# Weight parts at turning start bytes in a float32r transformer layer

## The chip, the cores and the metric

The kernel runs on one core of one Trainium2 chip. The metric is the device time of one execution in microseconds (us). Three runs of the kernel before gave 1863.11, 1863.22 and 1865.91 us; the median is 1863.22 us. The profile comes from one more execution, which took 1856.3 us.

On the core, TensorE multiplies matrices. A matmul has a stationary operand, which is loaded first by a weight load, and a moving operand, which streams past it. The profile shows the matmuls as PE and the weight loads as PEld. ACT (ScalarE) and DVE (VectorE) do elementwise work, POOL (GpSimd) and SP (SyncE) mostly issue DMAs. Operands lie in the on-chip memory with 128 partitions; a tile takes the same bytes of every partition.

## The reference, cut to what matters

One transformer layer over 512 tokens with 2048 features: attention in a window of 128 tokens, then a swiglu with 5632 inner features.

```
h = rms_norm(x, mixer_norm)
x = x + sliding_window_attention(h, positions, w_qkv, q_norm, k_norm, sinks, w_o)
h = rms_norm(x, ffn_norm)
x = x + (silu(h @ w_gate) * (h @ w_up)) @ w_down
```

Everything is float32.

## The kernel before, in words

**Split products.** Every large product is done in float32r, a form of float32 that TensorE takes in one pass. Each operand is split into a high part (ACT copies the value, rounded to float32r) and a low part (DVE subtracts the high part from the value). A product is then three matmuls: high by high, high by low, low by high. All weight tiles come from memory by DMA as float32 and are split this way, and TensorE reads only the parts. `copy_r` and `sub` are the two helpers, so most rows of the profile for splits stand under their lines (L65 for ACT, L70 for DVE), and nearly all matmuls stand under the line of `mm` (L144).

**Stages.** The program goes in this order:

1. The qkv projection and the attention, interwoven by a table of events. Here the activations (`hhi`, `hlo`) are stationary and the weight parts (`whi`, `wlo`) move, 512 columns at a time.
2. The output projection. Its last 512 columns use eight pairs of weight parts that have their own pool: `ohi` and `olo`, 8 buffers each. They are made in `w_split`. Again the activations are stationary and the weight parts move. This stage has 4 token tiles of 16 row tiles of 3 matmuls, so 192 matmuls of 512 columns.
3. The first two units of the gate, with whole weight tiles (`whi`, `wlo` stationary, `hhi`, `hlo` moving).
4. The swiglu proper, from `unit` and `s_split`. It uses a fast matrix product of seven instead of eight block products. There are 168 steps. In each, `s_split(i)` makes a pair `Whi`, `Wlo` of [128, 2, 7, 128] in two buffers by turns, and TensorE does 2 x 7 x 3 = 42 matmuls with 128 weight columns stationary and 256 moving columns. So the stage has 168 x 42 = 7056 matmuls. Three of the seven products have `hhi`, `hlo` as the moving operand (18 of the 42 matmuls), four have the combinations `sh0` to `sh3` and `sl0` to `sl3` (24 of the 42).
5. The down projection, in three passes over the inner features, four times 512 output columns each. `d_split` makes the parts `dwh`, `dwl` of [128, 7, 256] in three buffers by turns. Here the activation is stationary (`sh`, `sl` in the first four steps of a pass and column group, `hhi`, `hlo` in the rest) and the weight parts move. For the first 512 columns of a pass the product is plain, with 24 matmuls of 512 moving columns a step; for the others it is the fast form, with 42 matmuls of 256 moving columns a step. That makes 288 matmuls with `sh`, `sl` and 240 with `hhi`, `hlo` of 512 columns, and 1512 and 1260 of 256 columns.

**Order.** TensorE's order is written out by hand throughout, and ACT's and DVE's from the last output columns on. Tiles in the pools are placed one after the other from a base address; a few `place` tiles in the down projection fix which tile lands where, so that early ones lie where the swiglu's buffers are already free.

**Where the parts begin.** All row lengths before are multiples of 512 bytes, so every part of one kind begins at the same byte modulo 512. In the built program these bytes are:

| Stage | stationary operand, byte modulo 512 | moving operand, byte modulo 512 |
|---|---|---|
| last output columns | `hhi`, `hlo`: 352 | `ohi`, `olo`: 480 |
| first gate units | `whi`, `wlo`: 352 | `hhi`, `hlo`: 352 |
| swiglu | `Whi`, `Wlo`: 352 | `hhi`, `hlo`: 352; `sh`, `sl`: 480 |
| down projection | `hhi`, `hlo`: 352; `sh`, `sl`: 480 | `dwh`, `dwl`: 352 |

A tile of 128 float32r columns is 512 bytes wide, so one weight load reads 512 bytes of a partition; 256 moving columns are 1024 bytes, 512 are 2048.

In the attention the transposes of the probabilities `p` have `p` itself as the stationary operand; its rows are 132 numbers long, so its blocks begin at eight different bytes, 16 apart (160 to 272 modulo 512).

Of the kernel before, what the change touches and what calls it, by code (L numbers as in the profile page):

```python
# [11 lines left out]
F32R = mybir.dt.float32r  # L12
# [7 lines left out]
P = 128  # L20
# [26 lines left out]
def hybrid_layer(ctx, tc, x, positions, inv_freq, mixer_norm, ffn_norm, w_qkv, q_norm, k_norm, sinks,  # L47
# [15 lines left out]
    def copy_r(dst, src, scale=None):  # L63
        if scale is None:
            act.activation(dst, src, AF.Copy)  # L65
        else:
            act.activation(dst, src, AF.Copy, scale=scale)  # L67

    def sub(dst, a, b):
        dve.tensor_tensor(dst, a, b, ALU.subtract)  # L70
# [26 lines left out]
    st = {"dma": 0, "spl": 0}  # L97
    last_o = [None]

    def w_dma(upto):  # L100
        while st["dma"] < min(upto, len(wlist)):
            i = st["dma"]
            raw = wp.tile([P, 2, 512], F32, tag="wraw", name="wraw", bufs=NRAW)
            nc.sync.dma_start(raw, wlist[i])
            wtiles[i] = raw
            st["dma"] += 1

    def w_split(upto):
        while st["spl"] < min(upto, len(wlist)):
            i = st["spl"]  # L110
            raw = wtiles[i]
            if i == 0 and "w0" in st:
                split0(1)
                wtiles[0] = st.pop("w0")
                st["spl"] += 1
                continue
            if N_F - 8 <= i < N_F:
                p_, tg, nb = last_o[0], "o", 8
            else:
                p_, tg, nb = wp, "w", NSPL  # L120
            hi = p_.tile([P, 2, 512], F32R, tag=tg + "hi", name=tg + "hi", bufs=nb)
            lo = p_.tile([P, 2, 512], F32R, tag=tg + "lo", name=tg + "lo", bufs=nb)
            for k in range(2):
                copy_r(hi[:, k, :], raw[:, k, :])
                sub(lo[:, k, :], raw[:, k, :], hi[:, k, :].bitcast(F32))
            wtiles[i] = (hi, lo)
            st["spl"] += 1

    def split0(k):

        if k == 0:
            st["w0"] = [wp.tile([P, 2, 512], F32R, tag=n, name=n, bufs=NSPL) for n in ("whi", "wlo")]
        hi, lo = st["w0"]
        copy_r(hi[:, k, :], wtiles[0][:, k, :])
        sub(lo[:, k, :], wtiles[0][:, k, :], hi[:, k, :].bitcast(F32))

    def w_ahead(i):

        w_dma(i + 3)
        w_split(i + (3 if i > 4 else 1))  # L140
        w_dma(i + 5)
# [73 lines left out]
    for n in range(1, 8):  # L215
        x_slab(nc.sync, n, 0, 4)
        w_dma(min(n + 1, 3))
# [37 lines left out]
    for i in range(5):  # L255
        ev(i - 0.48, lambda i=i: w_split(i + 1))
# [98 lines left out]
    for j in range(5):  # L355
        for kk in range(8):
            i = 8 * j + kk
# [254 lines left out]
    for n, (c, kk) in enumerate(OORDER):  # L612
        i = N_O + n
# [38 lines left out]
    for c, bk, tm in ((1, 1, 54), (0, 4, 56), (2, 2, 64)):  # L652
        for t in range(NT):
            ev(tm - 0.0005, lambda c=c, bk=bk, t=t: o_evac(c, ob[bk], t))

    ev(N_F - 7.9, lambda: (w_dma(N_F + 4), w_split(N_F + 3)))

    for n in range(8):
# [127 lines left out]
    for kk in range(NH, 8):  # L786
        i = N_F + kk
# [9 lines left out]
    fp = fpx.enter_context(tc.tile_pool(name="ffn", bufs=1, reuse_waits="tile"))  # L797
# [23 lines left out]
    def s_sums(upto):  # L821
        while sw["sum"] < min(upto, len(steps)):
            W = stiles[sw["sum"]]
            sub(W[:, :, 4:6, :], W[:, :, 1:3, :], W[:, :, 0:1, :].to_broadcast([P, 2, 2, P]))
            dve.tensor_tensor(W[:, :, 6, :], W[:, :, 2, :], W[:, :, 4, :], ALU.add)
            sub(W[:, :, 7, :], W[:, :, 6, :], W[:, :, 3, :])
            sw["sum"] += 1

    def s_split(i):

        if i < len(steps):
            W = stiles[i]
            hi = fp.tile([P, 2, 7, P], F32R, tag="Whi", name="Whi", bufs=2)
            lo = fp.tile([P, 2, 7, P], F32R, tag="Wlo", name="Wlo", bufs=2)
            copy_r(hi, W[:, :, 1:8, :])
            s_sums(i + 2)
            sub(lo, W[:, :, 1:8, :], hi.bitcast(F32))
            stiles[i] = (hi, lo)
# [82 lines left out]
    gs = []  # L921
    s_sums(1)
    s_split(0)
    for u in range(2):
        G = gtile(u)
# [34 lines left out]
    def sum_tile():  # L960
        return dp.tile([P, 4, 256], F32, tag="sum", name="sums")
# [9 lines left out]
    for n in ("raw0", "dw0", "dwh0", "dwl0", "raw1", "dw1", "dw2", "dwh1", "sum", "dwl1"):  # L971
        n_, r_ = {"ra": (1024, F32), "dw": (1024, F32), "su": (1024, F32)}[n[:2]]
        if n[:3] in ("dwh", "dwl"):
            n_, r_ = 1792, F32R
        dp.tile([P, n_], r_, tag=n, name="place")
    opnd = [operand(v) for v in range(8)]

    def split(hi, lo, src):
        copy_r(hi, src)
        sub(lo, src, hi.bitcast(F32))  # L980
# [15 lines left out]
    def d_split(upto):  # L996
        while dw["spl"] < min(upto, len(dsteps)):
            i = dw["spl"]
            ps, c, v = dsteps[i]
            W, rs = draw.pop(i)  # L1000
            W = W.rearrange("p k (f c) -> p (k f) c", c=256)
            n = i % (3 if dp2[0] else 2)
            p_ = dp2[0] if n == 2 else dp
            hi = p_.tile([P, 7, 256], F32R, tag=f"dwh{n}", name="dwh")
            lo = p_.tile([P, 7, 256], F32R, tag=f"dwl{n}", name="dwl")
            if c == 0:
                oh, ol = opnd[v]
                T = sum_tile()
                dve.tensor_tensor(T[:, 0, :], rs[:, 1, :], rs[:, 3, :], ALU.add)
                sub(T[:, 1, :], T[:, 0, :], rs[:, 0, :])  # L1010
                sub(T[:, 2, :], rs[:, 0, :], rs[:, 1, :])
                sub(T[:, 3, :], rs[:, 2, :], T[:, 1, :])
                split(hi[:, 0:4, :], lo[:, 0:4, :], W)
                split(oh[:, 0:4, :], ol[:, 0:4, :], rs)
                split(oh[:, 4:8, :], ol[:, 4:8, :], T)
            else:
                T = sum_tile()
                sub(T[:, 0:2, :], W[:, 1:3, :], W[:, 0:1, :].to_broadcast([P, 2, 256]))
                dve.tensor_tensor(T[:, 2, :], W[:, 2, :], T[:, 0, :], ALU.add)
                sub(T[:, 3, :], T[:, 2, :], W[:, 3, :])  # L1020
                split(hi[:, 0:3, :], lo[:, 0:3, :], W[:, 1:4, :])
                split(hi[:, 3:7, :], lo[:, 3:7, :], T)
            dtiles[i] = (hi, lo)
            dw["spl"] += 1
# [29 lines left out]
    def d_ahead(i, n=3):  # L1054
        d_dma(i + 2)
        d_split(i + n if dp2[0] else i + 2)
        d_dma(i + 4)
# [57 lines left out]
    i = 0  # L1115
# [82 lines left out]
```

## Time and profile before

| What | us |
|---|---|
| median of three runs | 1863.22 |
| profiled execution, device time | 1856.3 |
| its span, from the first to the last instruction | 1854.5 |
| PE busy | 1837.2 |
| PEld busy | 1719.8 |
| DVE busy | 1489.4 |
| ACT busy | 874.6 |

The profiled execution lies 6.9 us under the median of the three runs, and 1.8 us of it lie outside the span. TensorE is busy nearly all the time. Since matmuls are pipelined, a busy PE does not say that it works at its peak: the useful number is the time from the start of one matmul to the start of the next, which is called the pace below. It is read from stretches without a pause, as the time of a stretch divided by its number of matmuls.

### The profile page before, as it was taken

The page shows a single profiled execution, that of the slowest core. Times are in us where ns is not written, and L with a number is a line of the kernel's source. Part 1 is how long each engine was busy: PE and PEld are TensorE (multiplying, and loading weights), DVE is VectorE, ACT ScalarE, POOL GpSimd, SP SyncE. Part 2 cuts the span into 40 slices and gives each one's busy share as a digit, 9 for nine tenths or more (in the row PEclk, how much of TensorE's full clock was granted, in tenths as well). Part 3 has the DMA queues.
Part 4 walks back from the last instruction along what each step waited for, and adds up shares of the span by engine and source line. Part 5 has one row for each costly group of instructions (what it writes and reads, how often), then busy time and mean ns, then how long its engine had stood idle before and what let it go on. Part 6 is the DMA issues. An engine that isn't in the chain of part 4 may idle for free.

```text
span 1854.5 us, 32562 instructions
## 1 busy us (share of the span) xinstructions
PE 1837.2 (99%) x13119; PEld 1719.8 (93%) x13119; DVE 1489.4 (80%) x2341; ACT 874.6 (47%) x1315; POOL 153.4 (8%) x215
## 2 busy tenths in 40 slices
PE   9999999999999999999999999999999999999999
PEld 7888778788889999999999999999998999999899
DVE  5568797764687888888888888888889888988987
ACT  6468788753454333334343343433435434534532
POOL 0013123120000000000000000000000111012011
PEclk9999999999999999999999999999999999999999
DMA  6321211144413333333333333333436556646665
GB/s 207 102 80 58 67 59 58 58 142 164 166 50 104 127 116 124 126 120 120 114 124 116 127 125 114 119 121 114 135 116 209 157 132 161 185 125 153 164 184 136
DMA packets 162950, 230.81 MB, mean 124 GB/s; under 512 B 10124, under 2 KB 109520, under 8 KB 162288
## 3 DMA queue, kind: packets, MB, share of 16 engines
q1 hardware_dynamic: 146656, 195.07, 32.9%
q0 software_dynamic: 15552, 32.61, 7.7%
q8 instruction: 102, 1.67, 0.4%
q10 hardware_dynamic: 592, 1.07, 0.2%
q14 instruction: 48, 0.39, 0.1%
HBM read 200.39 MB, written 31.46 MB: 125 GB/s over the span
## 4 chain that ended last, share of the span: by engine, by line
PE 88%; DVE 8%; ACT 2%; issue 1%; DMA 1%; POOL 0%; ACTq 0%; DVEq 0%; POOLq 0%
PE acc L144 84%; DVE wlo L70 1%; PE sc L144 1%; PE po L144 1%; DVE qraw L340 1%; DVE hlo L70 1%; DVE dwl L70 1%; ACT p L520 0%; DVE qss L443 0%; PE pT L531 0%; DVE sums L70 0%; DVE pl L70 0%; PE pt L699 0%; PE pt L249 0%; DMA raw<-actd 0%
## 5 line engine op out<-in xcount | busy, mean ns | idle before, releaser
L65 ACT ACTIVATE Whi<-W 128x1792 fp32r<-128x1792 f32 x168 | 286.3, 1704 | 503.3 <-PE acc L144 320.5
L70 DVE TENSOR_TENSOR Wlo<-W,Whi 128x1792 fp32r<-128x1792 f32 x168 | 340.2, 2025 | 117.9 <-ACT Whi L65 117.4
L144 PE MATMUL acc<-sl,Whi 128*128 128x256 f32 x1344 | 377.7, 281 | 0.0
L144 PE MATMUL acc<-sh,Whi 128*128 128x256 f32 x1344 | 377.4, 281 | 0.0
L144 PE MATMUL acc<-sh,Wlo 128*128 128x256 f32 x1344 | 372.7, 277 | 0.0
L144 PE MATMUL acc<-hhi,Wlo 128*128 128x256 f32 x1008 | 283.4, 281 | 0.6 <-DVE Wlo L70 0.6
L144 PE MATMUL acc<-hhi,Whi 128*128 128x256 f32 x1008 | 283.6, 281 | 0.0
L144 PE MATMUL acc<-hlo,Whi 128*128 128x256 f32 x1008 | 281.6, 279 | 0.0
L144 PEld LDWEIGHTS acc<-sh,Whi 128*128 128x128 f32 x1344 | 252.7, 188 | 0.0
L144 PEld LDWEIGHTS acc<-sh,Wlo 128*128 128x128 f32 x1344 | 252.5, 188 | 0.0
L144 PEld LDWEIGHTS acc<-sl,Whi 128*128 128x128 f32 x1344 | 252.3, 188 | 0.0
L144 PE MATMUL acc<-whi,hhi 128*128 128x512 f32 x512 | 208.7, 408 | 0.8 <-ACT hhi L67 0.8
L144 PE MATMUL acc<-whi,hlo 128*128 128x512 f32 x512 | 201.7, 394 | 0.1
L144 PE MATMUL acc<-wlo,hhi 128*128 128x512 f32 x512 | 200.7, 392 | 0.0
L70 DVE TENSOR_TENSOR W<-W 128x512 f32<-128x512 f32 x336 | 186.0, 554 | 7.5 <-DMA W<-ffn_w_up_in 0.9
L144 PEld LDWEIGHTS acc<-hhi,Wlo 128*128 128x128 f32 x1008 | 189.8, 188 | 0.8 <-DVE Wlo L70 0.8
L144 PEld LDWEIGHTS acc<-hhi,Whi 128*128 128x128 f32 x1008 | 189.4, 188 | 0.0
L144 PEld LDWEIGHTS acc<-hlo,Whi 128*128 128x128 f32 x1008 | 189.2, 188 | 0.0
L144 PE MATMUL acc<-dwh,sl 128*128 128x256 f32 (+1 forms) x600 | 180.1, 300 | 0.0
L144 PE MATMUL acc<-dwl,sh 128*128 128x256 f32 (+1 forms) x600 | 180.0, 300 | 0.0
L144 PE MATMUL acc<-dwh,sh 128*128 128x256 f32 (+1 forms) x600 | 179.8, 300 | 0.2 <-ACT row L65 0.2
L144 PE MATMUL acc<-dwh,hhi 128*128 128x256 f32 (+1 forms) x500 | 150.0, 300 | 0.0
(291 smaller groups left out, 3558.2 us busy)
## 6 DMA issues: line engine op xcount, KB each, us to landing
W<-ffn_w_up_in SPq DMA_DIRECT2D x176, 256.0 KB, 3.0
dw<-ffn_w_down_in SPq DMA_DIRECT2D x88, 512.0 KB, 3.9
W<-ffn_w_gate_in SPq DMA_DIRECT2D x160, 256.0 KB, 3.1
wraw<-attn_w_qkv_in SPq DMA_DIRECT2D x39, 512.0 KB, 3.7
wraw<-attn_w_o_in SPq DMA_DIRECT2D x32, 512.0 KB, 3.6
actd<-U POOLq DMA_DIRECT2D x22, 512.0 KB, 3.5
raw<-actd SPq DMA_DIRECT2D x22, 512.0 KB, 4.6
x1d<-row POOLq DMA_DIRECT2D x44, 256.0 KB, 5.7
```

The source lines that it names most:

```text
L65: act.activation(dst, src, AF.Copy)
L70: dve.tensor_tensor(dst, a, b, ALU.subtract)
L144: pe.matmul(ps, lhsT, rhs, start=start, stop=stop, skip_group_check=True)
L340: dve.tensor_tensor(s3, s3, t1[:, t, :].unsqueeze(1).to_broadcast([P, nh, HD]), ALU.mult)
```

## The change

No instruction is added or taken away, and on each engine the order is the same in both built programs. What changes is where tiles begin:

- **swiglu**: the two parts of step i are views into tiles that are 128 numbers longer, and begin 32 x (5 i mod 16) bytes later. Over 16 steps each multiple of 32 in a row of 512 bytes is used once.
- **last output columns**: each `ohi` and `olo` buffer is 16 numbers (64 bytes) longer, so that the 16 of them begin at 8 places, 64 bytes apart.
- **down projection**: `dwl0` is 64 bytes longer, which moves the tiles behind it, and `dwh2` is a view 64 bytes into a longer tile. The pairs of the three buffers then begin at bytes 352, 416 and 480.

The stationary and moving operands that are activations stay where they were, and so do all other stages. The waits of the instructions are the same but for two on ACT at the start of the down projection: the third `dwh` of the down projection now also waits until the swiglu's matmuls are over, and a copy of a result no longer waits for four earlier DMAs.

```
+    SHIFTS = 16
+
+    def shifted(tile_, i, n):
+
+        s_ = 8 * (5 * i % SHIFTS)
+        return tile_[:, s_:s_ + n]
...
-            hi = p_.tile([P, 2, 512], F32R, tag=tg + "hi", name=tg + "hi", bufs=nb)
-            lo = p_.tile([P, 2, 512], F32R, tag=tg + "lo", name=tg + "lo", bufs=nb)
+            hi, lo = [p_.tile([P, 1024 + (16 if tg == "o" else 0)], F32R, tag=tg + n_, name=tg + n_, bufs=nb)
+                      [:, 0:1024].rearrange("p (k c) -> p k c", c=512) for n_ in ("hi", "lo")]
...
-            hi = fp.tile([P, 2, 7, P], F32R, tag="Whi", name="Whi", bufs=2)
-            lo = fp.tile([P, 2, 7, P], F32R, tag="Wlo", name="Wlo", bufs=2)
+            hi, lo = [shifted(fp.tile([P, 1792 + SHIFTS * 8], F32R, tag=n_, name=n_, bufs=2), i, 1792)
+                      .rearrange("p (a s c) -> p a s c", a=2, c=P) for n_ in ("Whi", "Wlo")]
...
-            n_, r_ = 1792, F32R
+            n_, r_ = 1792 + (16 if n == "dwl0" else 0), F32R
...
-            hi = p_.tile([P, 7, 256], F32R, tag=f"dwh{n}", name="dwh")
-            lo = p_.tile([P, 7, 256], F32R, tag=f"dwl{n}", name="dwl")
+            hi, lo = [p_.tile([P, 1792 + (0, 0, 16)[n] if t_ == "dwh" else 1792 + (16, 0, 0)[n]], F32R, tag=t_ + str(n), name=t_)
+                      [:, (16 if n == 2 and t_ == "dwh" else 0):][:, 0:1792].rearrange("p (s c) -> p s c", c=256)
+                      for t_ in ("dwh", "dwl")]
```

## The prediction, made before the changed kernel was timed

> **What bounds the kernel now.** I read the busy times first, then the waits of TensorE, then the chain that ended last, cut to stretches, and last the durations of single groups of matmuls.
>
> The first lines are of TensorE's waits over the whole span (engine and line, what it waited for, us in total, times, longest). The only row of a stage that the change touches, but for one of 0.2 us, is the 0.6 us at the first step of the swiglu.
>
> ```profile
> PE po L144 <- DVE pl L70: 6.4, 3, 2.5
> ...
> PE acc L144 <- DVE Wlo L70: 0.6, 1, 0.6
> ```
>
> The next lines are the windows of the last output columns with the first gate units, of the swiglu, and of the down projection (length, then each engine's busy us and count, the granted clock, DMA).
>
> ```profile
> 469.00:566.00 97.00, 96.96 (x504) 82.32 (x503) 69.97 (x150) 44.61 (x86) 3.77 (x7) 1.00 0.29 103
> 566.00:1397.00 831.00, 830.43 (x7051) 830.23 (x7050) 701.78 (x935) 327.79 (x235) 11.19 (x21) 1.00 0.38 121
> 1397.00:1855.00 458.00, 453.12 (x3305) 430.59 (x3303) 393.09 (x554) 195.90 (x217) 53.08 (x49) 1.00 0.60 160
> ```
>
> In the swiglu the granted clock is 1.00, matmuls and weight loads are both busy for 830 of 831 us, and DVE for 702. So nothing arrives late; the time there is the number of matmuls times their pace. The pace is what a shifted weight part could change. I take it from pieces of the chain (start, us, what, count), one stretch in each fence. First the swiglu:
>
> ```profile
> 599.90 780.15 PE acc L144 x6624
> ```
>
> 780.15 / 6624 = 117.8 ns per matmul of 256 columns. Then the first gate units (512 columns; weights and moving operand both begin at byte 352):
>
> ```profile
> 539.94 25.16 PE acc L144 x111
> ```
>
> 25.16 / 111 = 226.7 ns. The last output columns (512 columns; stationary at 352, moving at 480):
>
> ```profile
> 469.83 17.03 PE acc L144 x73
> ```
>
> 17.03 / 73 = 233.3 ns. In the down projection with 256 columns, three stretches: `sh` stationary (480 against 352), `hhi` stationary (352 against 352), and `sh` again, in the second pass:
>
> ```profile
> 1446.94 14.60 PE acc L144 x123
> ```
> ```profile
> 1462.97 18.12 PE acc L144 x151
> ```
> ```profile
> 1601.45 19.08 PE acc L144 x159
> ```
>
> These are 118.7, 120.0 and 120.0 ns. For its 512 columns the first rows of three blocks of 96 matmuls (4 steps of 24) in the timeline of TensorE:
>
> ```profile
> 1397.33 0.39 PE L144 MATMUL acc<-dwh,sh 128*128 128x512 f32 x1
> ...
> 1419.63 0.39 PE L144 MATMUL acc<-dwh,hhi 128*128 128x512 f32 x1
> ...
> 1441.41 0.29 PE L144 MATMUL acc<-dwh,sh 128*128 128x256 f32 x1
> ```
>
> With `sh` (128 bytes apart) 22.30 us / 96 = 232.3 ns, with `hhi` (same byte) 21.78 / 96 = 226.9 ns. The two blocks run the same code with other stationary tiles, and what sets those apart for a read is where they begin, so **the distance between the operands' start bytes does matter**: apart costs 5.4 ns more at 512 columns, and 1.3 ns less or nothing at 256. The reader should keep that the sign turns with the width.
>
> What is the least pace? Between the matmuls of the last output columns stand transposes with 128 columns, where the moving operand is only half as long and the weight load paces:
>
> ```profile
> 486.86 1.75 PE pt L699 x16
> ```
>
> 1.75 / 16 = 109.4 ns. So a weight load can follow a weight load every 109.4 ns, and a matmul of 256 columns at 117.8 ns carries 8.4 ns that are neither: the most that the swiglu can gain is 8.4 ns x 7056 = 59 us.
>
> Within the swiglu the same instruction has more than one duration (minimum/median/maximum in ns, of the groups that read `Whi` and `Wlo`):
>
> ```profile
> L144 PE MATMUL acc<-sl,Whi x1344: 279/279/287, 565.9 to 1397.1; 128*128 128x256 f32 x192
> ...
> L144 PE MATMUL acc<-hlo,Whi x1008: 274/282/282, 565.5 to 1396.7; 128*128 128x256 f32 x168
> ...
> L144 PE MATMUL acc<-sh,Wlo x1344: 274/280/282, 566.0 to 1397.2; 128*128 128x256 f32 x192
> ```
>
> 274 and 287 both occur while the bytes modulo 512 are the same for all of a group. So the start bytes alone do not fix what a matmul pays; what came before it counts too. By these rows the good case is 274, some 6 to 7 ns under the median.
>
> **The change part by part.** It adds and moves no instruction. There are four terms.
>
> *Swiglu.* Before, 18 of 42 matmuls have both operands at one byte and 24 have them 128 apart. After it, each distance that is a multiple of 32 comes in one step of 16, so the share with the same byte falls from 43% to 6%. Two of the sixteen distances (0 and 128) stand in rows above, the other fourteen in none. From below, the pace cannot be under 109.4 ns (59 us less); from above, I take the 5.4 ns that the 512 columns pay for being apart, on all matmuls: 38 us more. The nearest rows are those with 256 columns and operands apart: 118.7 ns with `sh` stationary, and 117.8 ns for the swiglu's mixture itself. I take the middle, 118.25 ns: 0.45 ns x 7056 = **3.2 us more**.
>
> *Last output columns.* 192 matmuls now at 233.3 ns. One eighth comes to the same byte, at 226.8; the rest stays apart, at a price like the present one: 24 x 6.5 ns = **0.2 us less**. Between all at 226.8 (1.2 us less) and 5.4 ns more (1.0 us more).
>
> *Down projection.* With three places, each operand pair is at the same byte in one step of three. `hhi` loses it in two thirds: 840 matmuls of 256 columns x 1.3 ns less = 1.1 us less, 160 of 512 columns x 5.4 ns = 0.9 us more. `sh` gains it in one third: 504 x 1.3 = 0.7 us more, 96 x 5.4 = 0.5 us less. The sum is **0.0 us**. If the distance of 64 bytes, which none of the rows above has, were as good as 109.4 ns for half of the 2772 matmuls, it would give 14 us; at 5.4 ns more for them, it would cost 7 us.
>
> *Splits and waits.* ACT and DVE write the parts at the new bytes. Their rows show one place only, so the price is open, but it is covered: DVE has 701.78 us of work in 831, that is 4.18 us in a step of 4.95 us (42 x 117.8 ns), so a step may cost 0.77 us more before TensorE waits. I count **0**. The new wait of the third `dwh` is for matmuls that end at the row of 1397.33 above, and that split starts later:
>
> ```profile
> 1401.31 1.06 ACT L65 ACTIVATE dwh<-dw 128x1024 fp32r<-128x1024 f32 x1
> ```
>
> So it costs nothing either. If ACT held there, the next splits of the down projection would be queued behind it, and TensorE waits for those.
>
> The sum is 3.2 - 0.2 + 0.0 = 3.0 us more than the profiled 1856.3 us. That execution lies 6.9 us under the median; the change is the same in both, so by the median it is 1863.2 + 3.0 = **1866 us**.
>
> A rule that speaks against the whole change stands in the Trainium skill, "SBUF — State Buffer", section "Who interferes with whom": TensorE has two independent read ports, one for the moving operand and one for weight loads, and never waits on anyone. By it the start byte could cost nothing, the sum would be 0, and the time 1863 us. The rows of 232.3 and 226.9 ns differ with nothing but the place of the stationary operand, so the trace does not bear it out.
>
> **The rivals.**
>
> *The place of stationary weights alone does not matter.* The change does not reach the pace in the swiglu, and the time stays 1863 us. For it: the transposes of `p` have stationary operands at eight different bytes, those of `xn` always at one, and the durations are the same:
>
> ```profile
> L531 PE MATMUL pT<-ident,p x128: 270/272/273, 129.3 to 397.4; 128*128 128x128 f32 x128
> ...
> L699 PE MATMUL pt<-ident,xn x64: 270/272/278, 486.7 to 525.8; 128*128 128x128 f32 x64
> ```
>
> Against it: there the moving operand needs only half as long as the weight load, so there is room to hide a stall.
>
> *The reads come apart and the swiglu is faster.* If a weight load and the moving operand stall each other when they begin at distances of a multiple of 128, as all distances in the swiglu now are, then most of the new distances are better. The rows with 274 ns show that such a stall can be absent. At some 6 ns less for half of the matmuls it gives 3528 x 6 ns = 21 us less: 1842 us. It decides if the median durations of the groups above fall towards 274. By the Trainium skill, "TensorE: Matmul & The Clock Gate", section "Back-to-back issue gap", a warm matmul of 512 columns should follow the last after 215.8 ns; the trace has 226.9 to 233.3. By that rule all that lies above it could be had, which for 256 columns (109.2 ns there) is an estimated 61 us.
>
> *The new distances are worse.* At 512 columns, apart is 5.4 ns dearer than together. If that holds in the swiglu for half of the distances, 3528 x 5.4 ns = 19 us more: 1882 us. It decides in the swiglu's steps with odd multiples of 32, which stand for half of the steps and for no row of the trace. For it: the two blocks of 512 columns. Against it: at 256 columns, apart is not dearer in any row.
>
> **How the numbers follow.** This kernel's measurement can tell about 0.2%, 3.7 us, from no change. The forecast, an average over many distances that lands near the present mixture, has a chance of 0.42; 1866 us lies 3 us over the median, and the case spreads some 5 us around that, so I give 0.18 of it to within 0.2%, 0.19 to slower and 0.05 to faster. No effect at all: 0.12. The faster rival: 0.30, to which the 512-column rows do not speak. The slower one: 0.16. That makes faster 0.35, same 0.30, slower 0.35. The range reaches to the slower rival's 1882 us, and a little past the faster one's 1842, to 1838 us (7 ns in place of 6 on 3528 matmuls). It leaves out their far parts, about 2 in 10.
>
> **What would show it.** In the changed profile, the swiglu's piece of the chain divided by its count is the forecast's test: 118.2 ns or so. Under 116.5 the faster rival holds, above 119.5 the slower one, 117.8 with the same minima and maxima the one of no effect. Step by step, the pace of 42 matmuls should differ with a period of 16 steps. The last output columns should take 192 x 232.5 ns, 0.2 us less. In the down projection the `hhi` stretches should come down from 120.0 towards 118.7 ns at 256 columns and go up from 226.9 towards 230 at 512, `sh` the other way. It would be wrong if TensorE came to wait in the swiglu for `Wlo`, or if stages before 469 us changed.

## The result and the profile after

The changed kernel took 1850.71, 1853.56 and 1854.55 us in three runs, median 1853.56 against 1863.22 us before; the ratio is 0.994, with a 95% interval of 0.9918 to 0.9963. In a second comparison, on another chip, it was 1853.14 against 1859.27 us, ratio 0.9965 (0.9948 to 0.9983). So it is faster, by 0.6 and 0.35%; both intervals lie below 1. The forecast was 1866 us.

The profile moved far less than the median. The profiled execution of the changed kernel took 1853.56 us, that of before 1856.3 us: 2.7 us less, where the medians of the first comparison are 9.7 us apart. TensorE's waits after the change (columns as before; `mm` stands at L152 in the changed kernel, eight lines further down) are the same two rows in the stages that it touches:

```profile
PE acc L152 <- DVE Wlo L70: 0.6, 1, 0.6
...
PE acc L152 <- ACT row L65: 0.2, 1, 0.2
```

The windows of the last output columns with the first gate units, of the swiglu, and of the down projection:

```profile
469.00:566.00 97.00, 96.96 (x504) 82.47 (x503) 70.30 (x150) 44.92 (x87) 3.78 (x7) 1.00 0.29 103
566.00:1397.00 831.00, 830.43 (x7045) 830.23 (x7044) 699.83 (x935) 327.75 (x235) 11.23 (x21) 1.00 0.38 120
1397.00:1855.00 458.00, 450.40 (x3310) 427.27 (x3308) 393.63 (x554) 196.78 (x218) 53.10 (x49) 1.00 0.60 160
```

In the same 831 us TensorE starts 7045 matmuls, where it started 7051 before. The pace of the swiglu can be read from its long piece of the chain:

```profile
599.90 780.11 PE acc L152 x6618
```

780.11 / 6618 = 117.9 ns, after 117.8. On average the swiglu is as it was. The windows of the swiglu as a whole and of the three stretches of 256 columns in the down projection, cut at the first matmul of each, give the sum. Before:

```profile
565.39:1397.33 831.94, 831.37 (x7058) 831.17 (x7057) 702.11 (x936) 328.20 (x235) 11.19 (x21) 1.00 0.38 120
1441.41:1562.18 120.77, 120.57 (x1009) 120.35 (x1008) 101.42 (x141) 49.93 (x57) 14.51 (x14) 1.00 0.55 140
1600.80:1706.17 105.37, 105.37 (x883) 105.36 (x882) 88.07 (x122) 43.53 (x51) 14.52 (x14) 1.00 0.56 141
1744.79:1850.04 105.25, 105.25 (x883) 105.25 (x881) 86.12 (x121) 39.53 (x46) 16.25 (x16) 1.00 0.63 159
```

After:

```profile
565.42:1397.99 832.57, 832.00 (x7057) 831.79 (x7056) 700.82 (x936) 328.60 (x235) 11.23 (x21) 1.00 0.38 120
1442.39:1561.82 119.43, 119.26 (x1010) 119.06 (x1008) 101.31 (x141) 50.13 (x57) 14.51 (x13) 1.00 0.55 142
1600.47:1704.49 104.02, 104.02 (x883) 104.01 (x882) 88.72 (x123) 44.62 (x51) 14.50 (x13) 1.00 0.57 143
1743.27:1847.29 104.02, 104.02 (x882) 104.02 (x881) 85.90 (x121) 39.58 (x46) 16.26 (x16) 1.00 0.63 161
```

The swiglu costs 0.6 us more (832.57 against 831.94). From the end of the swiglu to the end of the last stretch it was 1850.04 - 1397.33 = 452.7 us and is 1847.29 - 1397.99 = 449.3 us: 3.4 us less. Together that is close to the 2.7 us of the profiles. The last output columns, from their first matmul to their last (with the transposes between them), before and after:

```profile
469.21:518.93 49.72, 49.72 (x240) 41.00 (x239) 29.68 (x76) 20.82 (x45) 3.23 (x6) 1.00 0.34 131
```
```profile
469.45:518.96 49.51, 49.51 (x240) 40.98 (x239) 29.76 (x76) 20.86 (x45) 3.24 (x6) 1.00 0.34 131
```

That is 0.2 us less.

The other 6.9 us of the 9.7 are the distance of the profiled execution of before from the median of its runs. The reader needs one plain fact here: **the times of the kernel before fall into two groups**, whatever the chip. Of the 91 runs of it that stand beside the experiments below, 39 are under 1859 us (the short group, median 1854.85), 50 are over 1861.9 us (the long group, median 1863.85), and two lie between. The share differs from chip to chip (17 of 35 short ones on one, 10 of 13, 4 of 23, 1 of 11 and 7 of 9 on others), and so a ratio to before depends on it. The granted clock does not set them apart: two runs of the repeat `b_again` took 1854.49 and 1862.87 us, both at a granted clock of 0.998. The profile shown before is of a short one, and the three runs beside it are long ones. The changed kernel's 15 times form one group, 1850.4 to 1856.8 us. So the question for the experiments was what the long group is, and why the change removes it.

### The profile page after: what moved, and what is told of

It is laid out like the page before. It is cut to its first block, busy times and chain, and to the rows that moved or that the text cites. A ratio compares the mean times of both kernels' runs of the same rounds, so it can differ in the third digit from the quotient of the medians.

```text
span 1851.8 us, 32561 instructions
## 1 busy us (share of the span) xinstructions
PE 1834.6 (99%) x13119; PEld 1716.5 (93%) x13119; DVE 1488.4 (80%) x2341; ACT 876.1 (47%) x1315; POOL 153.7 (8%) x215
## 4 chain that ended last, share of the span: by engine, by line
PE 88%; DVE 8%; ACT 2%; issue 1%; DMA 0%; POOL 0%; DVEq 0%; POOLq 0%; ACTq 0%
PE acc L152 85%; DVE wlo L70 1%; PE sc L152 1%; PE po L152 1%; DVE hlo L70 1%; DVE dwl L70 1%; DVE qraw L348 0%; PE pT L539 0%; DVE sums L70 0%; DVE pl L70 0%; DVE qss L451 0%; ACT p L528 0%; PE pt L707 0%; PE pt L257 0%; DMA raw<-actd 0%
## 5 line engine op out<-in xcount | busy, mean ns | idle before, releaser
L152 PE MATMUL acc<-sh,Whi 128*128 128x256 f32 x1344 | 376.8, 280 | 0.0
L152 PE MATMUL acc<-sl,Whi 128*128 128x256 f32 x1344 | 376.7, 280 | 0.0
L152 PE MATMUL acc<-sh,Wlo 128*128 128x256 f32 x1344 | 376.6, 280 | 0.0
L152 PE MATMUL acc<-hhi,Wlo 128*128 128x256 f32 x1008 | 282.2, 280 | 0.6 <-DVE Wlo L70 0.6
L152 PE MATMUL acc<-hlo,Whi 128*128 128x256 f32 x1008 | 282.7, 280 | 0.0
L152 PE MATMUL acc<-hhi,Whi 128*128 128x256 f32 x1008 | 282.4, 280 | 0.0
L152 PEld LDWEIGHTS acc<-sh,Whi 128*128 128x128 f32 x1344 | 253.5, 189 | 0.0
L152 PEld LDWEIGHTS acc<-sl,Whi 128*128 128x128 f32 x1344 | 252.9, 188 | 0.0
L152 PEld LDWEIGHTS acc<-sh,Wlo 128*128 128x128 f32 x1344 | 252.6, 188 | 0.0
L152 PE MATMUL acc<-whi,hhi 128*128 128x512 f32 x512 | 208.8, 408 | 0.8 <-ACT hhi L67 0.8
L152 PE MATMUL acc<-whi,hlo 128*128 128x512 f32 x512 | 201.7, 394 | 0.1
L152 PE MATMUL acc<-wlo,hhi 128*128 128x512 f32 x512 | 200.7, 392 | 0.0
L152 PEld LDWEIGHTS acc<-hhi,Wlo 128*128 128x128 f32 x1008 | 189.8, 188 | 0.8 <-DVE Wlo L70 0.8
L152 PEld LDWEIGHTS acc<-hhi,Whi 128*128 128x128 f32 x1008 | 189.8, 188 | 0.0
L152 PEld LDWEIGHTS acc<-hlo,Whi 128*128 128x128 f32 x1008 | 189.6, 188 | 0.0
L152 PE MATMUL acc<-dwh,sh 128*128 128x256 f32 (+1 forms) x600 | 179.1, 298 | 0.2 <-ACT row L65 0.2
L152 PE MATMUL acc<-dwh,sl 128*128 128x256 f32 (+1 forms) x600 | 178.9, 298 | 0.0
L152 PE MATMUL acc<-dwl,sh 128*128 128x256 f32 (+1 forms) x600 | 178.9, 298 | 0.0
L152 PE MATMUL acc<-dwh,hhi 128*128 128x256 f32 (+1 forms) x500 | 149.6, 299 | 0.0
```

What stands on the lines that cost most here:

```text
L152: pe.matmul(ps, lhsT, rhs, start=start, stop=stop, skip_group_check=True)
```

## The experiments

A word that they use: the *distance* is the number of bytes by which the stationary operand begins further on than the moving one, modulo 256. All bytes are given modulo 512.

**One part alone, and repeats.** `b_again` is the kernel before and `a_again` the changed one, unchanged. `swi_only` has only the swiglu's part of the change, `down_only` only the down projection's:

```
swi_only:
...
+            hi, lo = [shifted(fp.tile([P, 1792 + SHIFTS * 8], F32R, tag=n_, name=n_, bufs=2), i, 1792)
+                      .rearrange("p (a s c) -> p a s c", a=2, c=P) for n_ in ("Whi", "Wlo")]
...
down_only:
+            n_, r_ = 1792 + (16 if n == "dwl0" else 0), F32R
...
+            hi, lo = [p_.tile([P, 1792 + (0, 0, 16)[n] if t_ == "dwh" else 1792 + (16, 0, 0)[n]], F32R, tag=t_ + str(n), name=t_)
...
```

> The kernel before, unchanged. Its three timed runs took 1863 to 1866 us and its profiled execution 1856.3 us, a gap of 7 us, while the changed kernel's profiled execution is one of its three runs (1853.56 us). Theory A (the swiglu has two standing rhythms at the same start bytes, and an execution falls into one or the other): some executions take about 1856 us and others about 1863 us, and a profile of a long one shows a swiglu pace near 118.8 ns instead of 117.8 ns. Rival B (the gap comes from the stages before 469 us, from the clock or the DMAs): the swiglu's pace is 117.8 ns in every profile, and what differs lies in the first quarter. Rival C (another chip or another hour): all executions of this submission agree within 3 us.

> Only the swiglu's sixteen places; the last output columns and the down projection as before. From the two profiles (swiglu 831.9 us before, 832.6 us after): a profile against the profile before differs by -1 to +2 us. If theory A holds, the places by turns take the chance out of the swiglu, and the median lies some 3 to 7 us under that of a kernel before that falls into the slow rhythm; if rival B or C holds, the ratio is 0.999 to 1.002.

> Only the down projection's three places. From the two profiles the down projection gains 3.3 us (256 columns: -1.3 us in each of three passes; 512 columns together +0.5 us): the time is 3 to 4 us less than the kernel before in the same rhythm, a ratio of 0.998, and a pace of 114.1 ns stands at sh stationary with the weight parts at byte 416. If the gain came from the swiglu instead, this kernel is the same as the one before within 1 us.

> The changed kernel, unchanged: a ratio of 0.994 again if the first comparison was typical of the kernel before; 0.998 if the kernel before runs at 1856 us here. The profile again shows 117.9 ns in the swiglu, with a pattern that repeats every 8 of the 16 places.

| run | median us | lowest to highest | ratio to before (95%) |
|---|---|---|---|
| `b_again` | 1861.73 | 1854.49 to 1867.44 | 1.0001 (0.998 to 1.0022) |
| `swi_only` | 1856.91 | 1854.22 to 1859.18 | 0.9977 (0.9959 to 0.9995) |
| `down_only` | 1862.63 | 1855.80 to 1866.55 | 1.0013 (0.9993 to 1.0034) |
| `a_again` | 1853.14 | 1850.41 to 1856.83 | 0.9965 (0.9948 to 0.9983) |

With the swiglu's turning places the long group is gone, without them it is there. The traces of `swi_only` and `a_again` have 832.57 us in the swiglu, as the changed kernel's has, and in all three the pace of a step goes through the same pattern every 8 steps, from 116.4 to 119.05 ns. The 3.8 us between the medians of `swi_only` and `a_again` are the rest of the change; by the profiles it is 3.4 us in the down projection and 0.2 us in the last output columns. The repeat of before did not bring a trace of a long execution, so the two rhythms of theory A were not yet seen.

`down_only` gained nothing, for a reason of its own. In its waits DVE (`sums`) holds for TensorE, and TensorE later for DVE; neither row is in the changed kernel's waits:

```profile
DVE sums L1010 <- PE acc L144: 4.8, 1, 4.8
```
```profile
PE acc L144 <- DVE dwl L70: 2.5, 1, 2.5
```

Without the swiglu's longer tiles, the down projection's `sums`, 64 bytes further on, reaches 64 bytes into the last `Wlo`, so DVE may not write it before the swiglu's last matmuls have read that `Wlo`. The window of its first 512-column block shows what that cost, and the next one what the places gained:

```profile
1397.26:1425.92 28.66, 25.56 (x99) 20.04 (x97) 28.15 (x44) 16.53 (x17) 0.00 (x0) 0.88 0.64 202
1447.99:1567.00 119.01, 119.01 (x1010) 119.01 (x1008) 98.41 (x137) 47.90 (x55) 14.44 (x13) 1.00 0.55 138
```

The block takes 28.7 us for 22.3, at a granted clock of 0.88 on average, and the 256-column stretch 119.0 us for 120.8. So the whole time of this run does not judge the down projection's part; `no_turn` below does.

**Every distance by itself.** `scan16` walks through 32 places 16 bytes apart, five steps at each, and makes `hhi` and `sh` begin at the same byte, so that a step has one distance:

```
+    def shifted(tile_, i, n):
+        s_ = 4 * (i // 5 % 32)
+        return tile_[:, s_:s_ + n]
...
+    cpool.tile([P, 32], F32, name="pad")
```

> The kernel before, with the swiglu's weight parts at 32 places 16 bytes apart (each place held for five steps of the list in turn), and a tile of 128 bytes put behind sl, so that both kinds of moving operand (hhi and sh) begin at byte 352 of a row of 512; no work is left out. Theory D (what counts is the distance of the stationary operand's first byte from the moving one's, and it repeats every 256 bytes): the pace of the 256-column matmuls is 114.1 ns at a distance of +64, 117.9 at -64, 118.6 at 128 and about 119.7 at 0, as the changed kernel's down projection has them, and the same again 256 bytes further. Rival P (the stationary operand's own byte counts): the pace by that byte is the one that the changed kernel's swiglu shows, 119.1 at byte 352, 116.4 at 416, 118.3 at 480, 118.6 at 256, whatever moves. Rival N (start bytes count for nothing, and the differences of half a per cent are noise of the clock): 117.9 at all places.

The windows of five steps (210 matmuls) each, at the distances +48, +64, +80, 128, again +48 and +64 (256 bytes further on), -64, and 0:

```profile
639.89:664.63 24.74, 24.74 (x213) 24.74 (x211) 21.20 (x28) 9.97 (x7) 0.00 (x0) 1.00 0.35 107
664.63:688.43 23.80, 23.80 (x212) 23.80 (x211) 20.07 (x28) 10.47 (x8) 0.53 (x1) 1.00 0.42 133
688.43:713.38 24.95, 24.95 (x213) 24.95 (x211) 22.06 (x30) 9.01 (x6) 0.53 (x1) 1.00 0.40 127
763.49:788.69 25.20, 25.20 (x212) 25.20 (x211) 20.91 (x28) 9.49 (x7) 0.53 (x1) 1.00 0.40 126
1036.79:1061.53 24.74, 24.74 (x213) 24.74 (x211) 21.11 (x28) 9.97 (x7) 0.00 (x0) 1.00 0.34 107
1061.53:1085.33 23.80, 23.80 (x212) 23.80 (x211) 20.60 (x29) 10.48 (x8) 0.53 (x1) 1.00 0.42 133
1260.43:1285.17 24.74, 24.74 (x213) 24.74 (x212) 20.97 (x30) 10.44 (x8) 0.53 (x1) 1.00 0.40 129
1358.80:1384.00 25.20, 25.20 (x213) 25.20 (x211) 20.99 (x29) 9.49 (x7) 0.53 (x1) 1.00 0.41 128
```

Divided by 210 these are 117.8, 113.3, 118.8, 120.0, 117.8, 113.3, 117.8 and 120.0 ns. Theory D expected 114.1 ns at +64, 117.9 at -64 and 119.7 at 0, each within 0.8 ns; at 128 it missed (118.6). The table repeats after 256 bytes to a hundredth of a microsecond. Rivals P (116.4 ns at byte 416) and N (117.9 everywhere) fall. The mean over all distances is no better than the old mixture: the swiglu takes 834.7 us, the one run 1858.19.

**One distance held.** `fix64` puts `Whi` and `Wlo` 64 bytes further on in all steps; `one64` adds the tile behind `sl`, so that every distance in the swiglu is the good +64:

```
+    def shifted(tile_, i, n):
+        s_ = 16
+        return tile_[:, s_:s_ + n]
one64 also:
+    cpool.tile([P, 32], F32, name="pad")
```

> The kernel before, with all the swiglu's weight parts 64 bytes further on (byte 416 instead of 352, in tiles that are 512 bytes longer); no turning, no work left out. Theory D: 18 of 42 matmuls stand at a distance of +64 from hhi (114.1 ns) and 24 at -64 from sh (117.9), mean 116.2 ns, so the swiglu takes about 821 us where the change takes 832.6, and the whole some 1843. Rival P: 116.4 ns, the same within 1 us. Rival N: 117.9 ns, 832 us, 1854 to 1863 in all. Theory A (the kernel before has two standing rhythms at its one place): whichever it is in, the times of this kernel need not have two groups, since place and distances are others.

> As fix64, and a tile of 128 bytes put behind sl, so that sh begins at byte 352 as hhi does: every matmul of the swiglu has its stationary operand 64 bytes further on in a row of 512 than its moving one, and every one of the down projection has both at 352. Theory D: 114.1 ns for all 7056 of the swiglu, 805 us, and 119.7 to 120 in the down projection's 256-column parts, about as before; some 1827 in all. Rival P: 116.4 ns in the swiglu as in fix64, 821 us, some 1843 in all. Rival N: 832 us, 1854 to 1863 in all.

Their medians and traces missed what theory D gave them. `fix64`: median 1853.57 us, 1845.86 to 1857.02, ratio 0.9975 (0.9953 to 0.9996). `one64`: 1855.21, 1829.08, 1856.62 and 1861.39 us. The traced executions have 831.9 us in the swiglu, as before has. The same 750 us of it, in the kernel before and then in `one64`:

```profile
600.00:1350.00 750.00, 750.00 (x6371) 750.00 (x6370) 638.82 (x856) 294.30 (x208) 10.66 (x20) 1.00 0.38 122
```
```profile
600.00:1350.00 750.00, 750.00 (x6370) 750.00 (x6369) 639.06 (x853) 293.89 (x208) 10.66 (x20) 1.00 0.38 121
```

6371 and 6370 matmuls: 117.7 ns each, at bytes at which `scan16` has 113.3. And yet one of the four runs of `one64` took 1829 us, 2 us over theory D's 1827, and the shortest of `fix64` 1845.86, 3 us over its 1843; neither was traced. **The bytes alone do not set the pace.** The next suspect is the past: what rhythm TensorE was in when it came to these bytes. `b_look1`, the kernel before once more, fell in the short group (1853.83 us, swiglu 831.9) and shows the rhythm of 117.8 ns again.

> The kernel before, unchanged, once more with a profile. Theory A (two standing rhythms of the swiglu at its one place): if the execution falls in the group above 1860 us, its swiglu takes some 840 us at 119.0 ns a matmul, where the two profiles so far (1856.3 and 1854.5) have 831.9 at 117.8, and all else agrees within 1 us; if it falls in the group below 1860, 832 again and nothing is learnt. Rival B (the groups come from the stages ahead of the swiglu, or from the granted clock): the swiglu stays at 832 and the first 470 us are 7 us longer.

**The past, on purpose.** Three kernels differ from the ones above in where single steps begin, most of them the first ones. `hold119` is the kernel before, with tiles 512 bytes longer as in `fix64`, entered from byte 192, as the changed kernel comes to byte 352; `hold113` is `one64`, entered from distance +48, as `scan16` comes to +64; `re113` enters again in every eighth step. `no_turn` is the changed kernel with the swiglu's turning undone:

```
hold119:
+        s_ = 88 if i < 10 else 0
hold113:
+        s_ = 12 if i < 10 else 16
re113:
+        s_ = 12 if i < 10 or i % 8 == 0 else 16
no_turn:
-        s_ = 8 * (5 * i % SHIFTS)
+        s_ = 0 * i
```

> The kernel before, with the swiglu's weight parts of the first ten steps at byte 192 of a row of 512 and of all 158 that follow at byte 352, where the kernel before has all of them; no work left out. Theory A (the matmul's rhythm keeps what it fell into, and at the kernel before's one place two are possible): entered from byte 192, as the changed kernel enters it every time, the rhythm is that of 119.05 ns (375 periods of 13.33 ns for the 42 of a step) and stays for the rest of the stage, where the traced executions of the kernel before have 117.78 (371 periods) at the same bytes; the swiglu then takes some 840 us in place of 831.9, and the whole some 1862. Rival (the bytes set the pace, memory has no part): 117.8 ns, 832 us, 1854.

> As one64 (sh at byte 352), with the swiglu's weight parts of the first ten steps at byte 400 and of all that follow at 416. Theory A: entered from byte 400, the rhythm is the 113.33 ns that the run with 32 places shows at byte 416 every time, not the 117.78 in which the traced execution of one64 stands at the very same bytes; if it lasts, the swiglu takes some 800 us and the whole some 1822; if some stall knocks it out, it goes to 117.78 from there on, between 1822 and 1854. Rival (the bytes set the pace): as one64's trace, 117.8 ns, 832 us, 1854.

> As hold113, and every eighth step again at byte 400, so that the rhythm is entered anew. Theory A: 7 of 8 steps at 113.33 and one at about 117.8 ns, mean 113.9, some 804 us for the swiglu and 1826 in all, with a small spread from execution to execution. Rival: 117.8 ns, 832 us, 1854.

> The changed kernel with one part undone: the swiglu's weight parts are at their first place (byte 352) in all steps, in the changed kernel's longer tiles; the turning places of the last output columns and of the down projection stay. Theory A: the two rhythms of the kernel before are back, so its times lie in two groups some 9 us apart; each group lies some 3 us under that of the kernel before, which is what the down projection's places give in the profile (1.3 us in each of three passes, less some 0.5 in the 512-column blocks); the trace has 831.9 or 840 us for the swiglu and 119.4, 104.0 and 104.0 for the 256-column stretches. Rival (the changed kernel's gain is the down projection's, and the swiglu's turning gives nothing): its times are those of the changed kernel, one group about 1853.

| run | median us | lowest to highest | ratio to before (95%) |
|---|---|---|---|
| `hold119` | 1863.20 | 1862.11 to 1866.78 | 1.001 (0.9997 to 1.0024) |
| `hold113` | 1827.04 | 1825.81 to 1828.88 | 0.9815 (0.9795 to 0.9835) |
| `re113` | 1829.28 | 1828.85 to 1830.69 | 0.9829 (0.9806 to 0.9852) |
| `no_turn` | 1859.81 | 1854.75 to 1863.12 | 0.9984 (0.9971 to 0.9997) |

The windows of eight steps (336 matmuls) of `hold113` are of the last eight at +48, the first eight at +64, and eight near the end:

```profile
575.64:615.21 39.57, 39.57 (x338) 39.57 (x337) 31.50 (x41) 14.63 (x10) 0.54 (x1) 1.00 0.38 119
615.21:653.29 38.08, 38.08 (x338) 38.08 (x337) 33.46 (x46) 15.64 (x11) 0.54 (x1) 1.00 0.39 125
1281.61:1319.69 38.08, 38.08 (x338) 38.08 (x337) 33.48 (x46) 15.63 (x11) 0.53 (x1) 1.00 0.39 125
```

39.57 / 336 = 117.8 ns, then 38.08 / 336 = 113.3 ns from the first step to the last. `best` and `best2` below enter the swiglu in the same way, on two other chips, and their swiglu runs at 113.3 ns too; so it is not the chip that sets `hold113` apart from `one64`. The same for `hold119`, first at byte 192, then at 352:

```profile
578.53:618.10 39.57, 39.57 (x338) 39.57 (x337) 31.63 (x41) 14.60 (x10) 0.54 (x1) 1.00 0.38 120
618.10:658.10 40.00, 40.00 (x338) 40.00 (x337) 33.70 (x46) 15.54 (x11) 0.54 (x1) 1.00 0.38 119
1318.10:1358.10 40.00, 40.00 (x338) 40.00 (x337) 33.64 (x46) 15.53 (x11) 0.53 (x1) 1.00 0.37 119
```

40.00 / 336 = 119.05 ns, held for 158 steps at the bytes at which before's traces have 117.8. Its swiglu takes 840.4 us, and all its ten runs lie where the long group of before lies. And `no_turn`, with no trick at its entry, has the long group back, and its profile caught one such execution. Its window for the swiglu and for the first stretch of 256 columns in the down projection:

```profile
564.32:1405.16 840.84, 840.27 (x7057) 840.07 (x7056) 702.44 (x936) 328.19 (x235) 11.23 (x21) 1.00 0.38 119
1449.45:1568.46 119.01, 119.01 (x1009) 119.01 (x1008) 100.88 (x141) 50.09 (x57) 14.50 (x13) 1.00 0.55 141
```

840.84 us for 831.94 at unturned bytes: 8.9 us, the gap between the two groups (1863.85 - 1854.85 = 9.0). Its ten long runs have a median of 1860.0 us, 2.9 under the 1862.95 of the 19 long runs of before on that chip; some 3 were expected from the down projection's places. In the two rivals' terms: memory has a part, and the change's gain is not the down projection's alone. A long execution of the kernel before itself was not caught in a trace; that its swiglu takes some 840 us is concluded from `no_turn` and `hold119`.

**The same in the down projection, and the best of it.** The places that the change turns through in the down projection include a distance of +64 for `sh` (480 against 416). In the changed kernel's own trace, single steps (42 matmuls each) show it; the first four have `sh` at +64, 0, +128, +64:

```profile
1482.62:1487.40 4.78, 4.78 (x45) 4.78 (x43) 4.59 (x9) 0.94 (x2) 3.55 (x4) 1.00 0.78 102
1487.40:1492.42 5.02, 5.02 (x45) 5.02 (x43) 4.39 (x7) 2.77 (x3) 0.49 (x1) 1.00 1.11 179
1492.42:1497.41 4.99, 4.99 (x45) 4.99 (x44) 4.62 (x6) 1.92 (x2) 0.00 (x0) 1.00 0.49 155
1497.41:1502.18 4.77, 4.77 (x45) 4.77 (x43) 4.37 (x7) 1.91 (x2) 0.00 (x0) 1.00 0.46 148
```

113.8, 119.5, 118.8 and 113.6 ns. `best` is `hold113` with +64 throughout the down projection; `best2` moves one step in each pass to +48, so as to enter the rhythm there too (added lines only):

```
best:
+    sink_b = ap_.tile([P, 32], F32, name="sink_b")
+    mask = ap_.tile([P, P], U8, name="mask")
...
+    dp.tile([P, 48], F32, name="padd")
best2 also:
+        s_ = 12 if i < 4 else 16
...
+    identr = ap_.tile([P, P], F32R, name="identr")
...
+            n_, r_ = 1792 + (64 if n[3] == "0" else 0), F32R
...
+            s_ = 4 if i in (12, 42, 69) else 0
+            hi, lo = [p_.tile([P, 1792 + (64 if n == 0 else 0)], F32R, tag=f"{t_}{n}", name=t_)
+                      [:, s_:s_ + 1792].rearrange("p (s c) -> p s c", c=256) for t_ in ("dwh", "dwl")]
```

> hold113, and the same distance in the down projection: mask and sink_b, which only the attention uses, lie in the attention's pool instead of the one that lives to the end, and the 256 bytes that this frees go to a tile of 192 bytes ahead of the down projection's tiles, so that its moving operands (dwh, dwl) begin 64 bytes ahead of the stationary ones in a row of 256, where before and in hold113 they begin at the same byte. Theory A with distance (each distance has its rhythms, and at +64 the shortest is 113.33 ns): the 2772 matmuls of 256 columns go from 120.0 ns to between 113.3 and 114.1 if they fall into that rhythm (16 to 18 us less), or to 117.8 if they fall into the one of one64's trace (6 us less); the 528 of 512 columns go from 227.5 to some 233 ns, 3 us more. So 1811 to 1813 us in the first case and 1824 in the second; the swiglu stays at 802.4. Rival (the gain of the changed kernel's down projection comes from the turning itself, not from a distance that one of its places has): the 256-column parts stay at 121.4, 105.8 and 105.7 us and the whole at 1827.

> The run best, with the rhythm entered on purpose in the down projection as in the swiglu: one step in each of its three passes (the fifth of the first pass's 256-column steps, the fourth of the second's, the third of the last's) has its moving operands 16 bytes further on, at a distance of +48 in place of +64; and the swiglu's first four steps, in place of its first ten, are at 48. identr, which only the attention uses, lies in the attention's pool, which makes room for it. Theory A (the rhythm is kept until something breaks it, and from +48 to +64 it falls into 113.33 ns): behind those steps the 256-column matmuls run at 113.33 ns in place of best's 117.78, that is some 19 of 24 steps of the first pass, 17 of 21 and 18 of 21, 54 steps of 42 by 4.45 ns, 10.1 us less in the down projection; the swiglu's six steps give 1.1 us more; some 1811 us against the traced 1824.1 of best, and a narrow spread. Rival (entering works in the swiglu alone, since there the turning operand is the stationary one): the down projection stays at 118.7, 103.9 and 103.8 us, and the whole at best's.

`best`: median 1821.57 us (1812.86 to 1824.39), ratio 0.9762 (0.9738 to 0.9786). `best2`: 1814.28 us (1811.80 to 1817.33), ratio 0.9769 (0.9745 to 0.9792) to a before with more short runs on that chip. The three stretches of 256 columns, `best` and then `best2`:

```profile
1413.13:1531.86 118.73, 118.73 (x1010) 118.72 (x1009) 100.12 (x139) 49.84 (x57) 14.51 (x13) 1.00 0.55 139
1571.05:1674.93 103.88, 103.88 (x884) 103.88 (x882) 87.99 (x123) 43.72 (x51) 14.50 (x13) 1.00 0.57 143
1714.12:1817.88 103.76, 103.76 (x882) 103.76 (x881) 86.08 (x121) 39.32 (x46) 16.25 (x16) 1.00 0.64 161
```
```profile
1411.97:1526.48 114.51, 114.51 (x1009) 114.51 (x1008) 99.74 (x139) 50.22 (x57) 14.51 (x13) 1.00 0.55 144
1565.80:1666.58 100.78, 100.78 (x884) 100.78 (x883) 88.14 (x123) 44.28 (x51) 14.50 (x13) 1.00 0.58 147
1705.77:1808.24 102.47, 101.48 (x882) 100.95 (x881) 85.63 (x120) 38.46 (x45) 16.25 (x16) 1.00 0.63 162
```

In `best`'s trace these matmuls are at 117.8 ns (118.73 / 1008, 103.88 / 882), as in `one64`; one of its six runs is 11.3 us shorter than the traced one. In `best2` 114.51 / 1008 = 113.6 ns. The three stretches are 118.73 + 103.88 + 103.76 - 114.51 - 100.78 - 102.47 = 8.6 us shorter, where 10.1 were expected. Single steps of `best2` show how it came to that: of the first pass the first and the fifth (the one at +48), of the second pass the third, the fourth (at +48), the fifth and the sixth:

```profile
1411.97:1416.73 4.76, 4.76 (x43) 4.76 (x42) 4.40 (x7) 4.20 (x7) 2.61 (x4) 1.00 0.57 134
1431.02:1436.02 5.00, 5.00 (x45) 5.00 (x43) 4.57 (x8) 1.91 (x2) 0.00 (x0) 1.00 0.48 172
1575.69:1580.63 4.94, 4.94 (x44) 4.94 (x43) 4.51 (x8) 1.91 (x2) 0.00 (x0) 1.00 0.91 279
1580.63:1585.64 5.01, 5.01 (x45) 5.01 (x43) 4.51 (x7) 1.79 (x2) 0.00 (x0) 1.00 0.42 150
1585.64:1590.41 4.77, 4.77 (x44) 4.77 (x43) 3.54 (x5) 1.80 (x2) 0.00 (x0) 1.00 0.30 101
1590.41:1595.17 4.76, 4.76 (x44) 4.76 (x43) 3.70 (x6) 1.80 (x2) 0.00 (x0) 1.00 0.31 105
```

In the second pass the steps go from 117.8 ns over the one at +48 to 113.3 ns (4.76 / 42) and stay there, as theory A has it. But the first pass was at 113.3 ns from its first step on, ahead of its step at +48, and so was the third (4.77 us for its first step). So in the down projection entry by +48 is seen once; what put the other two passes into the short rhythm isn't shown. In the third pass three steps with pauses take 5.24, 5.50 and 5.91 us, together 2.4 us more than 3 x 4.76, and the steps behind them take 4.76 us again: those pauses did not break the rhythm. `best2`'s swiglu took 802.3 us, not the 1.1 us less than `hold113`'s 802.4 that was expected. The 512-column blocks pay for +64: the first takes 23.5 us for 21.8 in `hold113`, 1.1 us of that with a pause, and the one that opens the second pass, without a pause, 22.4 for 21.8.

**What stays open.** In all five traces with the swiglu's parts at byte 352 throughout (the kernel before, `b_again`, `b_look1`, `down_only`, `no_turn`) the swiglu's first step runs at 119.05 ns, and the second, in which TensorE waits for `Wlo`, is some 0.85 us longer than those that follow. These run at 117.78 ns in the first four and at 119.05 in `no_turn`. It fits that the moment at which this pause ends decides, but no run removed or shifted the pause, so that isn't shown. What part of the chip keeps time in this way isn't shown by any row.

## Why the prediction was wrong

- **"The change is the same in both"**: this step failed. It put the 6.9 us between the profiled execution and the median on the changed kernel as well. They were a property of the kernel before, whose profile was of a short execution and whose median was of long ones. The long ones have, by `no_turn` and `hold119`, another rhythm in the swiglu (840.8 and 840.4 against 831.9 us), and turning places remove it: all three traces with them have the same sum, 832.57 us, with the same paces every 8 steps, and the times form one group. The signs were there: the three runs lie within 2.8 us of each other and 6.8 us or more above the profiled one, the prediction itself says that "what came before it counts too", and two of its rows have `sh` at the same bytes at 118.7 and at 120.0 ns (14.60 / 123 and 19.08 / 159).
- **Swiglu, "3.2 us more"**: mis-sized; 0.6 us more in the trace, at 117.9 ns where 118.25 were taken. Against the long rhythm of `no_turn` it is 8.3 us less (840.84 - 832.57). The pace differs from step to step, as was said, but with a period of 8 steps, not 16, since the distances count modulo 256 bytes (`scan16`). The bounds of this term (59 us less to 38 us more) held what a better place can give: 831.9 - 802.4 = 29.5 us less in `hold113`.
- **Last output columns, "0.2 us less"**: held; 49.51 us for 49.72.
- **Down projection, "0.0 us"**: mis-sized; 3.4 us less. The pairs at 0 and 128 behaved about as taken. What was left out of the value, though it stood in the bound, is the distance of 64 bytes: the steps of `sh` at +64 run at 113.6 to 114.1 ns and those of `hhi` at -64 at 117.9, not at 118.7 to 120. Of the forecasts for the traces, the `hhi` stretches came down at 256 columns and up at 512 (22.2 us for a block of 21.8), and the `sh` blocks came down at 512 (22.2 for 22.3), as said. The `sh` stretches at 256 columns were to go up and came down: the four steps shown above take 19.56 us, where the stretch at that place (from 1482.01 us) took 19.93 before.
- **Splits and waits, 0**: held. The only wait in the swiglu is the same 0.6 us (it lies in the second step, not in the first as the prediction says), and DVE has 700.82 us for 702.11. The third `dwh` made nobody wait.
- **The rival of no effect** was closest by the profile's mean (117.9 ns for 117.8), and wrong: single steps run at 116.4 to 119.05 ns, and the median fell. The faster rival's mechanism, that most of the new distances are better, fell: the swiglu over 32 places in `scan16` takes 834.7 us, and the median durations, which were to fall towards 274 ns, are 280 ns in all six groups after the change. The slower rival fell with the swiglu's mean of 117.9 ns, under its limit of 119.5.
- **The rule from the Trainium skill** that spoke against the change ("SBUF — State Buffer", section "Who interferes with whom": TensorE has two independent read ports and never waits on anyone) does not speak of start bytes; as the prediction reads it, it gives one time for all of them. `scan16` has 113.3 to 120.0 ns by the distance alone, so the runs do not bear that reading out.
- **The estimate of 61 us** takes a gap that the Trainium skill ("TensorE: Matmul & The Clock Gate", section "Back-to-back issue gap") gives for an isolated matmul, not for a stream with a weight load before each matmul. The shortest pace that was held here is 113.3 ns, where that estimate takes 109.2.

## What to carry to other kernels

In this kernel a matmul stream without waits still had a pace that depends on how far apart the start bytes of the stationary and the moving operand lie, and it could be locked to one of several paces at the same bytes. In a kernel like it, look at the time of a whole repeated group, not at single durations, and compare it between stretches. Where runs of one kernel fall into two groups, find out which one the profile caught before its offset to the median is carried over to a change. Turning through places bought steadiness and the mean; choosing one good distance and coming to it from a place that leads into the good rhythm bought 1.9% here (1.5% against the short group's median), and 2.3% with the down projection's.

## What the runs showed that was not expected

- Paces are locked: in the stretches that ran longest at one pace, the time of a step of 42 matmuls is a whole number of periods of 13.33 ns. 117.78 ns is 371 of them (42 x 117.78 = 4946.8; 371 x 13.333 = 4946.5), 119.05 is 375, 113.33 is 357, 120.0 is 378. The period is read from these four alone, and not every place has a whole number: at +80 the five steps of `scan16` take 24.95 us, some 374.2 periods each. Kernels with quite different durations inside a step (112 to 124 ns from start to start in before, 117 to 119 in `one64`) have the same 371.
- The same pair of start bytes ran at 117.8 or 119.05 ns (352 against 352 and 480), and at 113.3 or 117.8 ns (+64), for over 150 steps on end, and the pauses and transfers of DVE, ACT and the DMAs within them did not change it.
- The pattern over places repeats every 256 bytes, and 16 bytes matter: 117.8, 113.3 and 118.8 ns at +48, +64 and +80. At 512 columns the order is another: 0 is the best (226.7 to 227.0 ns), and +64 (233.3 ns in `best`) costs about as much as 128 (232.3 to 233.3 ns in the kernel before).
